# Sparse-attention heads: values stationary in half of TensorE's columns, probabilities scaled first and moving, the result already transposed

## The chip, the cores and the metric

The kernel runs on one core of one Trainium2 chip, as a single launch. The metric is device time in microseconds (us). Three runs of the kernel before took 1006.0, 1002.8 and 1006.0 us; the median is 1006.0.

## What is computed

Two transformer blocks, one after the other, on 256 tokens of width 1024 in float32. The first has a state-space mixer, a latent attention and a gated FFN; nothing in it is changed. The second has two attention mixers side by side (a sparse one, called NSA, with 12 heads, and a dilated one with 12 heads), gates, output projections and a squared-relu FFN.

The change lies in the NSA mixer. Its 12 query heads are in 3 groups of 4; a group shares one key and value head of width 64 for each of three branches:

- compressed: 15 block summaries of keys and values;
- selected: with 256 tokens there are only 4 blocks of 64 and all of them are selected, so this is plain causal attention;
- window: the window of 512 covers all 256 tokens, so this too is plain causal attention, with keys and values of its own.

For each head `y = gate0 * o_cmp + gate1 * o_slc + gate2 * o_win`, where each `o` is `softmax(q k^T * scale) v`. The 12 heads' `y` (768 columns) then goes through `w_o_a`.

## The kernel before

All weights are streamed from HBM in blocks of up to 128x2048 float32, in two halves. Each half lands in `wraw` (3 buffers); ScalarE (ACT) rounds it to `whi`, VectorE (DVE) makes `wlo = wraw - whi` (5 buffers each). A product is then three float32r matmuls (hi*hi, hi*lo, lo*hi), accumulated in PSUM in a tile named `pa` (token-major, 128x384 or 128x512 moving) or `pb` (channel-major, 128x256 moving). These make up most of the program, and their activations are `hTh` and `hTl`.

Attention is done in plain float32. In the NSA part (lines 1511 to 1573, tile names in brackets) the program goes over 3 groups `g` and, in each, over 4 heads `r`:

- scores of both branches w = 0 (selected) and 1 (window), for token tiles tt = 0 and 1, in one PSUM tile (`psN`), mask and row maximum on DVE, exponential on ACT into `pr2` (the page writes `pr`), with the row sums in `dens`;
- the probabilities are transposed on TensorE (`trp2`, page `trp`): 6 transposes of 128x128 a head, copied out to `pT2` (page `pT`) by ACT or DVE;
- 6 matmuls a head (L1554 to 1559) with the transposed probabilities (128 keys x 128 tokens) stationary and the values `vtok` (page `vsw`, 64 columns) moving, into `po`: two PSUM tiles a group, token-major, each branch and head apart.

At the end of a group (L1560 to 1573) the sums are inverted and multiplied by the gates; for each token tile DVE multiplies `po` by that factor into `yt` (512 columns), adds the two branches (256 columns) and adds the compressed branch `yc` into `yA` (256 columns). `yc` comes from `pcv`: the compressed probabilities `pcm`, transposed (`trpc`, `pcT`), times the block-diagonal values `vbd`, two matmuls of 256 columns a group, copied out by ACT. `yA` is transposed by 4 more transposes a group (`trya`) and split into `yATh`, `yATl` for the output projection.

The order of the instructions is made by a planner, `_Plan` (L518 to 794). The program is first run dry; each instruction is noted with its engine, operands and an estimated length (`_cost`, L561 to 577). Then a list schedule is made: each engine takes, of the instructions whose operands and buffers are there, the one of the lowest rank. Ranks come from the table `RANK` (L40 to 48) by the stage's name: "nsa" by group, "cmp" for the block compression, "dil" for the dilated heads. A `copy` may go to ACT or DVE, whichever is free in the plan. All instructions are issued from one helper, hence one line number for all in the profile: L629.

PSUM has 8 banks in two tags: "acc" with 3 (`pa`, `pb`, `po`) and "g" with 5 (transposes and scores).

Of the kernel before, what the change touches and what calls it, by code (L numbers as in the profile page):

```python
# [9 lines left out]
F32 = mybir.dt.float32  # L10
# [7 lines left out]
P = 128  # L18
# [13 lines left out]
NARENA = 54  # L32
WRAW = 3
# [18 lines left out]
# ---------------------------------------------------------------- host layout  # L52
# [23 lines left out]
def _weights():  # L76
    """Blocks of the weight stream: (key, width, source array, builder)."""
# [89 lines left out]
def _consts():  # L167
    """Small constants: (key, width, builder of [128, width])."""
# [81 lines left out]
# ---------------------------------------------------------------- device side  # L250
# [9 lines left out]
class _Noted(Exception):  # L260
    """Leaves the context of the dry run before anything of it is compiled."""
# [20 lines left out]
def _body(plan, x_in, wts, cst, out):  # L282
# [6 lines left out]
    # ---- storage  # L289
    def a2(name, dtype=F32):  # L290
        return plan.tile("arena", [P, 512], dtype, name, "a", NARENA)

# [20 lines left out]
    # ---- weight stream  # L313
# [22 lines left out]
    # ---- constants and input  # L336
# [24 lines left out]
    # the tensor engine's clock rises with work: turned over until the input is there  # L361
# [15 lines left out]
    # ---- pieces  # L377
# [40 lines left out]
    def gain_T(xs, gain, name):  # L418
        """Transposes token-major k-tiles and multiplies them by their gains."""
# [8 lines left out]
    def norm_T(x, r, gain, name):  # L428
        """The normed x, transposed; r [P, 2]: the norm's factors per token."""
# [7 lines left out]
    def late_T(x, gain, name):  # L437
        """The gained x, transposed, and the mean squares per token [P, 2], by which the products with x are normed."""
# [13 lines left out]
    def spread(r):  # L452
        """Factors per token [P, 2] as a row [P, 256] on every partition."""
# [11 lines left out]
    def mmA(ps, act, tt, k0, nk, w, n, woffs, start, stop):  # L465
        """ps[128 tok, n] += act^T W for k-tiles k0.., weights block w at woffs(k)."""
# [9 lines left out]
    def mmB(ps, act, w, nk, woffs, k0=0):  # L476
        """ps[128 ch, 256 tok] = W^T act over nk k-tiles."""
# [8 lines left out]
    def chunkA(keys, act, n, kper):  # L486
        """Full-K token-major chunk over several blocks; returns the two psum tiles."""
# [16 lines left out]
    def mask_max(s, mask, mx):  # L504
        """s += mask, with the rows' maxima."""
# [13 lines left out]
class _Plan:  # L519
    """The order of the instructions. A first, dry run of the program notes every instruction with its engine, its  # L520
    length and what it reads and writes. From that a list schedule is made: each engine takes, of the instructions
    whose operands and buffers are there, the one of the lowest rank. The real run gives each instruction its place
    in that schedule as its priority."""
# [6 lines left out]
    # -- the dry run  # L530
# [16 lines left out]
    def either(self, *two):  # L547
        """An instruction that one of two engines runs."""
# [12 lines left out]
    def _cost(eng, op, outs, ins):  # L561
# [5 lines left out]
        if eng == "PE":  # L567
            n = outs[0].free_size()
            if op == "transpose":
                return max(n / 1.2, 107.0) + 2.5  # L570
            return (2 * max(n / 1.2, 107.0) if ins[0].dtype == F32 else max(n / 2.4, 107.0)) + 2.5
# [41 lines left out]
    # -- the real run  # L613
# [64 lines left out]
    def _run(self, graph, seq):  # L678
        """One pass; returns its length and every instruction's start. seq: the places of the weight blocks."""
# [117 lines left out]
class _Eng:  # L797
    """An engine whose instructions the plan notes. queue: the engine that starts it, where that is another."""
# [17 lines left out]
def _rope(V, dst, src, tc_, ts_, H, half, ta, tb):  # L816
    """dst[:, h, :] = rotated src[:, h, :]; tables [p, 2*half] with the gains folded in."""
# [8 lines left out]
def block1(env):  # L826
# [5 lines left out]
    # constants worked out on the chip  # L832
# [391 lines left out]
    # ---- FFN with the depthwise convolution  # L1224
# [33 lines left out]
def block2(env, x2):  # L1258
# [5 lines left out]
    # rope tables with the gains  # L1264
# [44 lines left out]
    def headnorm(ss, n):  # L1309
        """The factors of the heads' norms [P, 2 * n], the row's own included."""  # L1310
# [8 lines left out]
    # ---- compressed keys and values: transposed, second copy shifted by one token  # L1319
# [18 lines left out]
    # ---- selected and window keys  # L1338
# [71 lines left out]
    # ---- block compression  # L1410
# [100 lines left out]
    # ---- NSA by groups of four heads  # L1511
    yAT = S.hl("yAT", 3)
    for g in range(3):
        S.rank("nsa", g)
        yA = a2("yA").rearrange("p (t d) -> p t d", t=NTT)
# [5 lines left out]
        pcv = ps_s("pcv")  # L1521
        for tt in range(NTT):
            PE.matmul(pcv[:, tt * 256:(tt + 1) * 256], pcT[:, tt * P:(tt + 1) * P],
                      vbd[g].rearrange("p r d -> p (r d)"), start=True, stop=True)
        yc = a2("yc")
        S.copy(yc, pcv)
        den = small("dens", 16)
        denv = den.rearrange("p (t w h) -> p t w h", t=NTT, w=2)
        po = [S.ps_acc("po") for _ in range(NTT)]
        pov = [p_.rearrange("p (w h d) -> p w h d", w=2, h=4) for p_ in po]  # L1530
        for r in range(4):
            h = 4 * g + r
            prob = [a2("pr2") for _ in range(2)]
            for tt in range(NTT):
                nk = P * (tt + 1)
                s = ps_s("psN")[:, :2 * nk].rearrange("p (w b) -> p w b", w=2)
                for i in range(2):
                    PE.matmul(s, qT[h][:, tt * P:(tt + 1) * P], kT[g][i][:, :, 0:nk], start=i == 0, stop=i == 1)
                mx = small("mx2", 2)
                for w in range(2):  # L1540
                    S.mask_max(s[:, w], S.mcaus[:, 2 * P - nk:], mx[:, w:w + 1])
                nb = small("nb2", 2)
                V.tensor_scalar(nb, mx, sclA[:, h, tt:tt + 1], -1.0, op0=OP.mult, op1=OP.mult)
                for w in range(2):
                    A.activation(prob[tt][:, w * nk:w * nk + nk], s[:, w], AF.Exp, bias=nb[:, w:w + 1], scale=sclA[:, h, tt:tt + 1],
                                 accum_out=denv[:, tt, w, r:r + 1])
            pT = [a2("pT2") for _ in range(2)]
            for tt in range(NTT):
                pt = ps_tr("trp2")
                n = 256 * (tt + 1)  # L1550
                for i in range(n // P):
                    PE.transpose(pt[:, i * P:(i + 1) * P], prob[tt][:, i * P:(i + 1) * P], ident)
                S.copy(pT[tt][:, :n], pt[:, :n])
            for w in range(2):  # L1554
                vs = slice(g * 64, g * 64 + 64)
                PE.matmul(pov[0][:, w, r], pT[0][:, w * P:(w + 1) * P], vtok[w][0][:, vs], start=True, stop=True)
# [3 lines left out]
        V.reciprocal(den, den)  # L1560
        for w in range(2):
            V.tensor_tensor(denv[:, :, w], denv[:, :, w], gv[:, :, 4 * g:4 * g + 4, 1 + w], op=OP.mult)
        for tt in range(NTT):
# [5 lines left out]
        pt = ps_tr("trya").rearrange("p (a b) -> p a b", a=2)  # L1569
        for j in range(2):  # L1570
            for tt in range(NTT):
# [177 lines left out]
```

## Time and profile before

| what | value |
|---|---|
| three runs | 1006.0, 1002.8, 1006.0 us |
| span of the profiled execution | 1000.4 us |
| time around the span, by the median | 5.6 us |
| PE (TensorE) busy | 988.1 us, 99% |
| DVE busy | 782.5 us, 78% |
| ACT busy | 608.0 us, 61% |
| DMA, mean | 166 GB/s |
| NSA part, first score to last `po` matmul | 597 to 745 us |

The page gives the span of the profiled execution, from its first instruction to its last; the time of a run also has what lies around it, 2.4 to 5.6 us by the three runs. A float32 matmul appears as two records of the same shape, since TensorE makes two passes over it; a transpose and a float32r matmul appear as one. A record's duration is the time from its start until its results are written; the next one starts long before that, so what a matmul costs is the distance from its start to the next start, which the timeline shows: for n merged records, (merged time - one record) / (n - 1).

### The profile page before, as it was taken

Reading aid. Unit: us, or ns where it says so; the run is one execution under the profiler, and the core shown is the slowest. Engines: PE = TensorE matmul, PEld = TensorE weight load, DVE = VectorE, ACT = ScalarE, POOL = GpSimd, SP = SyncE. Lnnn points to the kernel's source line nnn. Section 1 sums busy time; section 2 is a strip of 40 time slices with the busy share of each in tenths; the row PEclk is TensorE's granted clock in tenths of the full one; section 3 lists DMA queues with packets and bytes.
Section 4 is the critical chain, followed back from the end, with each engine's and each line's share of the span. In section 5 each row is a group of like instructions: output and inputs, shape, how many; then the busy total and the mean of one; then the engine's idle time right before and its main releaser. Section 6 shows DMA issues by size and latency. Waiting matters only on the chain.

```text
span 1000.4 us, 18303 instructions
## 1 busy us (share of the span) xinstructions
PE 988.1 (99%) x6873; PEld 926.9 (93%) x6873; DVE 782.5 (78%) x1774; ACT 608.0 (61%) x1193; POOL 0.2 (0%) x4
## 2 busy tenths in 40 slices
PE   8999999999999999999999999999999999999998
PEld 7899988999999899999888998999989989998886
DVE  6897989989876779999855999989974866665442
ACT  5755879768644566666644767765674456554331
POOL 0000000000000000000000000000000000000000
PEclk9999999999999999999999999999999999999999
DMA  7655643235435455555555654365412645555561
GB/s 246 230 178 169 202 155 139 86 120 202 145 130 186 173 183 185 180 189 181 200 189 155 182 158 145 109 211 176 135 44 80 200 170 199 181 188 182 186 223 64
DMA packets 50536, 166.44 MB, mean 166 GB/s; under 512 B 5616, under 2 KB 6928, under 8 KB 50320
## 3 DMA queue, kind: packets, MB, share of 16 engines
q1 hardware_dynamic: 50448, 165.28, 49.1%
q8 instruction: 54, 0.88, 0.3%
q14 instruction: 34, 0.28, 0.1%
HBM read 164.18 MB, written 1.08 MB: 165 GB/s over the span
## 4 chain that ended last, share of the span: by engine, by line
PE 91%; DMA 3%; DVE 3%; ACT 1%; issue 1%; SPq 0%; DVEq 0%; ACTq 0%
PE pb L629 46%; PE pa L629 30%; DMA wraw<-in_wts_dram 3%; PE trp L629 2%; DVE wlo L629 1%; PE pob L629 1%; PE po L629 1%; PE py L629 1%; PE psS L629 1%; PE pov L629 1%; PE psD L629 1%; ACT whi L629 1%; PE psN L629 1%; PE trn L629 1%; PE trq L629 1%
## 5 line engine op out<-in xcount | busy, mean ns | idle before, releaser
L629 ACT ACTIVATE whi<-wraw 128x1024 fp32r<-128x1024 f32 (+3 forms) x318 | 321.3, 1011 | 290.4 <-PE pb L629 140.1
L629 DVE TENSOR_TENSOR wlo<-wraw,whi 128x1024 fp32r<-128x1024 f32 (+3 forms) x318 | 368.7, 1161 | 161.2 <-ACT whi L629 153.1
L629 PE MATMUL pb<-hTl,whi 128*128 128x256 f32 x1056 | 300.3, 285 | 0.0
L629 PE MATMUL pb<-hTh,whi 128*128 128x256 f32 x1056 | 300.1, 285 | 0.0
L629 PE MATMUL pb<-hTh,wlo 128*128 128x256 f32 x1056 | 300.0, 284 | 0.0
L629 PEld LDWEIGHTS pb<-hTl,whi 128*128 128x128 f32 x1056 | 202.4, 192 | 0.8 <-issue 0.6
L629 PEld LDWEIGHTS pb<-hTh,whi 128*128 128x128 f32 x1056 | 202.2, 192 | 0.8 <-issue 0.6
L629 PEld LDWEIGHTS pb<-hTh,wlo 128*128 128x128 f32 x1056 | 202.5, 192 | 0.4 <-issue 0.3
L629 PE MATMUL pa<-whi,uTh 128*128 128x512 f32 x216 | 84.2, 390 | 0.0
L629 PE MATMUL pa<-wlo,uTh 128*128 128x512 f32 x216 | 84.1, 390 | 0.0
L629 PE MATMUL pa<-whi,uTl 128*128 128x512 f32 x216 | 84.0, 389 | 0.0
L629 PE MATMUL pa<-wlo,hTh 128*128 128x384 f32 (+2 forms) x224 | 79.8, 356 | 0.0
L629 PE MATMUL pa<-whi,hTh 128*128 128x384 f32 (+2 forms) x224 | 79.5, 355 | 0.0
L629 PE MATMUL pa<-whi,hTl 128*128 128x384 f32 (+2 forms) x224 | 78.8, 354 | 0.0
L629 PEld LDWEIGHTS pa<-whi,uTl 128*128 128x128 f32 x216 | 40.6, 188 | 8.4
L629 PEld LDWEIGHTS pa<-wlo,uTh 128*128 128x128 f32 x216 | 40.5, 188 | 8.4
L629 PEld LDWEIGHTS pa<-whi,uTh 128*128 128x128 f32 x216 | 40.5, 188 | 8.3
L629 PEld LDWEIGHTS pa<-whi,hTl 128*128 128x128 f32 x224 | 42.2, 189 | 1.9
L629 PEld LDWEIGHTS pa<-whi,hTh 128*128 128x128 f32 x224 | 42.1, 188 | 1.9 <-ACT vbt L629 0.2
L629 PEld LDWEIGHTS pa<-wlo,hTh 128*128 128x128 f32 x224 | 42.1, 188 | 1.8
L629 DVE SCALAR_TENSOR_TENSOR fcv<-fpr,call,fcv 128x254 f32<-128x254 f32 (+1 forms) x88 | 38.5, 478 | 0.3 <-ACT fcv L629 0.3
L629 PE MATMUL pb<-ysTl,whi 128*128 128x256 f32 x128 | 37.1, 290 | 0.0
(397 smaller groups left out, 1752.3 us busy)
## 6 DMA issues: line engine op xcount, KB each, us to landing
wraw<-in_wts_dram SPq DMA_DIRECT2D x250, 512.0 KB, 4.2
wraw<-in_wts_dram SPq DMA_DIRECT2D x52, 384.0 KB, 3.2
dec<-aD SPq DMA_DIRECT2D x16, 256.0 KB, 5.4
wraw<-in_wts_dram SPq DMA_DIRECT2D x8, 256.0 KB, 2.7
wraw<-in_wts_dram SPq DMA_DIRECT2D x4, 448.0 KB, 4.3
wraw<-in_wts_dram SPq DMA_DIRECT2D x4, 420.0 KB, 3.8
call<-in_cst_dram SPq DMA_DIRECT2D x1, 1076.5 KB, 8.4
out_dram<-yo SPq DMA_DIRECT2D x3, 256.0 KB, 4.1
```

The costliest lines, as they stand in the source:

```text
L629: getattr(engines[eng], op)(*[swap(a) for a in args], **{k: swap(a) for k, a in kw.items()})
```

## The change

Four things are changed. The rest of the diff takes out comments and docstrings, which moves lines (the helper is L636 after).

1. The NSA heads are taken in pairs `j`. The sums of a head are inverted and multiplied by its gates as soon as its exponentials are done, and the probabilities are multiplied by that factor, in place, before they are transposed (`S.copy` with a scale, ACT or DVE). The same 6 transposes a head follow, now 3 to a PSUM tile and branch; the copies go to `pT2`, now a tile of 2 x 384 columns with 3 buffers of its own.
2. The values `vtok[w][kb][:, vs]` (64 columns) are the stationary operand. The transposed probabilities move: for key block kb = 0 all 256 tokens, for kb = 1 the later 128. Head 0 of the pair writes partitions 0 to 63 of `y`, head 1 partitions 64 to 127, so each matmul takes one half of the array's columns. Both branches and the compressed one (`vbd` stationary, `pcT` moving, 128 columns wide) accumulate in the same PSUM tile, which holds the transposed result and is split at once. `yt`, `yA`, `yc`, `pcv` and `trya` are gone.
3. The rank of "cmp" goes from 41.24 to 40.9.
4. `_cost` takes a float32 matmul whose stationary operand has 64 columns or 64 partitions as half as long as before.

```diff
+NPT = 3
...
-    "in2": [39.8, 45.14, 45.06, 55.07, 49.45], "cmp": [41.24], "nsa": [41.09, 41.19, 49.84], "qb": [46.71, 41.14],
+    "in2": [39.8, 45.14, 45.06, 55.07, 49.45], "cmp": [40.9], "nsa": [41.09, 41.19, 49.84], "qb": [46.71, 41.14],
...
+    def pt_tile(name):
+
+        return plan.tile("arena", [P, 2, 384], F32, name, "pT", NPT)
...
+            if ins[0].dtype == F32 and (ins[0].free_size() == 64 or ins[0].ap[0][1] == 64):
+                return n / 1.2 + 2.5
...
-        pcv = ps_s("pcv")
-        for tt in range(NTT):
-            PE.matmul(pcv[:, tt * 256:(tt + 1) * 256], pcT[:, tt * P:(tt + 1) * P],
-                      vbd[g].rearrange("p r d -> p (r d)"), start=True, stop=True)
-        yc = a2("yc")
-        S.copy(yc, pcv)
...
-        po = [S.ps_acc("po") for _ in range(NTT)]
...
+        y = S.ps_acc("po").rearrange("p (a b) -> p a b", a=2)
+        for j in range(2):
+            probs = []
+            for r in (2 * j, 2 * j + 1):
...
+                V.reciprocal(den, den)
+                V.tensor_tensor(denv, denv, gv[:, :, h, 1:3], op=OP.mult)
+                for tt in range(NTT):
+                    nk = P * (tt + 1)
+                    for w in range(2):
+                        S.copy(prob[tt][:, w * nk:w * nk + nk], prob[tt][:, w * nk:w * nk + nk], denv[:, tt, w:w + 1])
+                probs.append(prob)
+
+            PE.matmul(y[:, j], vbd[g][:, 2 * j:2 * j + 2].rearrange("p r d -> p (r d)"), pcT[:, :T], start=True, stop=False)
+            vs = slice(g * 64, g * 64 + 64)
+            for w in range(2):
+                pT = S.pt_tile("pT2")
                 for i in range(2):
...
+                    pt = ps_tr("trp2")
+                    for n, (tt, o) in enumerate(((0, w * P), (1, 2 * w * P), (1, (2 * w + 1) * P))):
+                        PE.transpose(pt[:, n * P:(n + 1) * P], probs[i][tt][:, o:o + P], ident)
+                    S.copy(pT[:, i], pt[:, :384])
...
                 for kb in range(2):
-                    o = w * 256 + kb * P
-                    PE.matmul(pov[1][:, w, r], pT[1][:, o:o + P], vtok[w][kb][:, vs], start=kb == 0, stop=kb == 1)
...
-        for tt in range(NTT):
-            t = a2("yt")
-            tv = t.rearrange("p (w h d) -> p w h d", w=2, h=4)
-            V.tensor_tensor(tv, pov[tt], denv[:, tt][:, :, :, None].to_broadcast([P, 2, 4, 64]), op=OP.mult)
-            V.tensor_tensor(t[:, :256], t[:, :256], t[:, 256:], op=OP.add)
-            V.tensor_tensor(yA[:, tt], t[:, :256], yc[:, tt * 256:(tt + 1) * 256], op=OP.add)
...
+                    for i in range(2):
+                        PE.matmul(y[64 * i:64 * i + 64, j, kb * P:], vtok[w][kb][:, vs],
+                                  pT[:, i, 2 * kb * P:(2 + kb) * P], start=False, stop=w == 1 and kb == 1)
+        S.split(yAT[g], y)
```

Up to some 600 us the built programs are the same on every engine. On PE, late in the NSA part of the kernel before, `po` matmuls (128 stationary columns, 64 moving) stand in small lots between transposes of the next heads:

```order
L629 MATMUL pb<-hTl,whi 128x256
L629 MATMUL po<-vsw,pT_9433 128x64 x2
L629 MATMUL trp_9451<-call,pr_9256 128x128 x3
L629 MATMUL po<-vsw,pT_9443 128x64 x4
L629 MATMUL trp_9464<-call,pr_9456 128x128 x2
L629 MATMUL trp_9451<-call,pr_9256 128x128
L629 MATMUL po<-vsw,pT_9448 128x64
```

On PE in the changed kernel, where the first group's results are formed, `vbd` (full width) opens each pair's half of `po`, and 8 matmuls on half the columns follow it, the two heads of the pair in turn:

```order
L636 MATMUL trpc<-call,pcm 128x128
L636 MATMUL po<-pcT,vbd 128x256
L636 MATMUL po<-pT_7975,vsw 64x256 x2
L636 MATMUL po<-pT_7975,vsw 64x128 x2
L636 MATMUL po<-pT_7988,vsw 64x256 x2
L636 MATMUL po<-pT_7988,vsw 64x128 x2
L636 MATMUL po<-pcT,vbd 128x256
L636 MATMUL po<-pT_8129,vsw 64x256 x2
L636 MATMUL po<-pT_8129,vsw 64x128 x2
L636 MATMUL po<-pT_8617,vsw 64x256 x2
L636 MATMUL po<-pT_8617,vsw 64x128 x2
L636 MATMUL trpc<-call,pcm 128x128
```

A `po` row says how many partitions are written (64 or 128) and how many columns move. The 48 half-width matmuls stand in 13 such unbroken stretches: three of 8, one each of 7, 4 and 3, three of 2 and four single ones. The `psD` matmuls (dilated scores, 64 rows) stand in 9 unbroken stretches before and in 7 after. All of group 0 now comes behind the block compression, since its accumulation begins with the compressed branch.

On DVE, at the first heads of the changed kernel, the inversion, the gates and the scaling stand between the score masks, the weights' low parts and the block compression (`hs`):

```order
L636 RECIPROCAL dens<-dens 128x4
L636 TENSOR_SCALAR nb_7933<-mx_7906,sclA 128x2
L636 TENSOR_TENSOR dens<-dens,gv 128x4
L636 ISA psN,mx_7912<-psN,mcaus 128x128
L636 ISA mx_7912 128x1
L636 TENSOR_SCALAR pr_7856<-pr_7856,dens 128x128
L636 TENSOR_SCALAR pr_7895<-pr_7895,dens 128x256
L636 TENSOR_TENSOR wlo<-wraw,whi 128x768
L636 TENSOR_SCALAR hs<-hs 128x180
```

Of the 48 scalings, 30 fall to DVE (17 of 128 columns, 13 of 256) and 18 to ACT (7 and 11).

## Rows read from the trace of the kernel before

**Rows 1.** The page, part 1: busy us (share of the span), instructions.

```profile
PE 988.1 (99%) x6873; PEld 926.9 (93%) x6873; DVE 782.5 (78%) x1774; ACT 608.0 (61%) x1193; POOL 0.2 (0%) x4
```

**Rows 2.** The page, part 4: the chain that ended last, by engine.

```profile
PE 91%; DMA 3%; DVE 3%; ACT 1%; issue 1%; SPq 0%; DVEq 0%; ACTq 0%
```

**Rows 3.** Busy time by stretch: stretch, us, PE, PEld, DVE, ACT, POOL, PEclk, DMA share, GB/s.

```profile
575.00:725.00 150.00, 146.97 (x1023) 141.25 (x1022) 141.37 (x453) 98.28 (x208) 0.00 (x0) 1.00 0.49 156
725.00:775.00 50.00, 50.00 (x398) 46.83 (x397) 30.09 (x103) 29.67 (x82) 0.00 (x0) 1.00 0.20 61
700.00:725.00 25.00, 25.00 (x193) 23.44 (x192) 24.19 (x95) 16.15 (x38) 0.00 (x0) 1.00 0.42 140
```

**Rows 4.** Waits of PE from 595 to 765: waited for, total us, times, longest.

```profile
PE trp L629 <- DVE qT L629: 0.9, 1, 0.9
PE po L629 <- ACT pT L629: 0.8, 2, 0.6
PE trq L629 <- DVE qT L629: 0.6, 1, 0.6
```

**Rows 5.** PE from 595 to 765, by shape: count, busy us, mean ns, idle before.

```profile
L629 PE MATMUL po<-vsw,pT 128*128 128x64 f32 x144 | 18.6, 270 | 0.8 <-ACT pT L629 0.8
L629 PE MATMUL pcv<-vbd,pcT 128*128 128x256 f32 x12 | 3.0, 388 | 0.0
```

**Rows 6.** Timeline of PE: start us, merged us, instruction, count.

```profile
629.83 3.68 PE L629 MATMUL po<-vsw,pT 128*128 128x64 f32 x32
...
713.59 1.89 PE L629 MATMUL pcv<-vbd,pcT 128*128 128x256 f32 x8
...
716.69 0.62 PE L629 MATMUL trya<-call,yA 128*128 128x128 f32 x4
```

**Rows 7.** Timeline of PE around matmuls of 64 rows (`psD`).

```profile
722.31 0.28 PE L629 MATMUL pb<-hTh,whi 128*128 128x256 f32 x1
722.52 0.93 PE L629 MATMUL psD<-qT,qT 64*128 64x128 f32 x6
...
723.61 0.28 PE L629 MATMUL pb<-hTh,wlo 128*128 128x256 f32 x1
```

**Rows 8.** Timeline of PE around matmuls of 45 and of 32 columns.

```profile
645.50 0.28 PE L629 MATMUL ph<-wlo,kps 128*45 128x256 f32 x1
645.62 0.28 PE L629 MATMUL ph<-whi,kps 128*90 128x256 f32 x1
645.74 0.28 PE L629 MATMUL ph<-wlo,kps 128*45 128x256 f32 x1
...
89.30 0.38 PE L629 MATMUL tra<-call,acum 128*32 128x128 f32 x2
89.43 0.48 PE L629 MATMUL pa<-whi,hTh 128*128 128x512 f32 x1
89.75 0.40 PE L629 MATMUL pa<-wlo,hTh 128*128 128x512 f32 x1
```

**Rows 9.** DVE from 590 to 765, by shape.

```profile
L629 DVE TENSOR_TENSOR yt<-po,dens 128x512 f32<-128x512 f32 x6 | 4.1, 686 | 0.4 <-PE po L629 0.2
L629 DVE TENSOR_TENSOR yt<-yt 128x256 f32<-128x256 f32 x6 | 2.5, 418 | 0.0
L629 DVE TENSOR_TENSOR yA<-yt,yc 128x256 f32<-128x256 f32 x6 | 2.3, 417 | 0.0
L629 DVE TENSOR_TENSOR dens<-dens,gv 128x8 f32<-128x8 f32 x6 | 0.8, 164 | 0.1
L629 DVE RECIPROCAL dens<-dens 128x16 f32<-128x16 f32 x3 | 0.8, 252 | 0.9 <-ACT pr L629 0.9
L629 DVE RECIPROCAL rdb<-rdb 128x8 f32<-128x8 f32 x1 | 0.2, 203 | 0.0
```

**Rows 10.** ACT, the same stretch.

```profile
L629 ACT ACTIVATE yc<-pcv 128x512 f32<-128x512 f32 x3 | 1.7, 595 | 0.8 <-PE pcv L629 0.8
```

**Rows 11.** Tiles `qn` and `junk`, nearest to the scalings: shortest, median, longest ns.

```profile
L629 DVE TENSOR_SCALAR qn<-qkv,ny x4: 283/316/349, 47.5 to 48.2; 128x256 f32<-128x256 f32 x2, 128x128 f32<-128x128 f32 x2
L629 ACT ACTIVATE junk<-qkv x6: 212/304/456, 27.5 to 35.0; 128x256 f32<-128x256 f32 x2, 128x128 f32<-128x128 f32 x2, 128x32 f32<-128x32 f32 x2
```

More of the change, by code (lines that the diff above doesn't have):

```diff
@@ L260 @@
 class _Noted(Exception):
+    pass
 def _net(tc, x_in, wts, cst, out):
@@ L1514, in block2 @@
         S.rank("nsa", g)
-        yA = a2("yA").rearrange("p (t d) -> p t d", t=NTT)
         ptc = ps_tr("trpc")
@@ L1520, in block2 @@
         S.copy(pcT[:, :256], ptc[:, :256])
-        pcv = ps_s("pcv")
-        for tt in range(NTT):
-            PE.matmul(pcv[:, tt * 256:(tt + 1) * 256], pcT[:, tt * P:(tt + 1) * P],
-                      vbd[g].rearrange("p r d -> p (r d)"), start=True, stop=True)
-        yc = a2("yc")
-        S.copy(yc, pcv)
-        den = small("dens", 16)
-        denv = den.rearrange("p (t w h) -> p t w h", t=NTT, w=2)
-        po = [S.ps_acc("po") for _ in range(NTT)]
-        pov = [p_.rearrange("p (w h d) -> p w h d", w=2, h=4) for p_ in po]
@@ L1531, in block2 @@
-        for r in range(4):
-            h = 4 * g + r
-            prob = [a2("pr2") for _ in range(2)]
-            for tt in range(NTT):
-                nk = P * (tt + 1)
-                s = ps_s("psN")[:, :2 * nk].rearrange("p (w b) -> p w b", w=2)
-                for i in range(2):
[L1538 to L1556, printed above, removed]
-                for kb in range(2):
-                    o = w * 256 + kb * P
-                    PE.matmul(pov[1][:, w, r], pT[1][:, o:o + P], vtok[w][kb][:, vs], start=kb == 0, stop=kb == 1)
@@ L1560, in block2 @@
[L1560 to L1563, printed above, removed]
-            t = a2("yt")
-            tv = t.rearrange("p (w h d) -> p w h d", w=2, h=4)
-            V.tensor_tensor(tv, pov[tt], denv[:, tt][:, :, :, None].to_broadcast([P, 2, 4, 64]), op=OP.mult)
-            V.tensor_tensor(t[:, :256], t[:, :256], t[:, 256:], op=OP.add)
-            V.tensor_tensor(yA[:, tt], t[:, :256], yc[:, tt * 256:(tt + 1) * 256], op=OP.add)
@@ L1569, in block2 @@
-        pt = ps_tr("trya").rearrange("p (a b) -> p a b", a=2)
-        for j in range(2):
-            for tt in range(NTT):
-                PE.transpose(pt[:, j, tt * P:(tt + 1) * P], yA[:, tt, j * P:(j + 1) * P], ident)
-        S.split(yAT[g], pt)
+        y = S.ps_acc("po").rearrange("p (a b) -> p a b", a=2)
+        for j in range(2):
+            probs = []
+            for r in (2 * j, 2 * j + 1):
+                h = 4 * g + r
+                prob = [a2("pr2") for _ in range(2)]
+                den = small("dens", 4)
+                denv = den.rearrange("p (t w) -> p t w", t=NTT)
+                for tt in range(NTT):
+                    nk = P * (tt + 1)
+                    s = ps_s("psN")[:, :2 * nk].rearrange("p (w b) -> p w b", w=2)
+                    for i in range(2):
+                        PE.matmul(s, qT[h][:, tt * P:(tt + 1) * P], kT[g][i][:, :, 0:nk], start=i == 0, stop=i == 1)
+                    mx = small("mx2", 2)
+                    for w in range(2):
+                        S.mask_max(s[:, w], S.mcaus[:, 2 * P - nk:], mx[:, w:w + 1])
+                    nb = small("nb2", 2)
+                    V.tensor_scalar(nb, mx, sclA[:, h, tt:tt + 1], -1.0, op0=OP.mult, op1=OP.mult)
+                    for w in range(2):
+                        A.activation(prob[tt][:, w * nk:w * nk + nk], s[:, w], AF.Exp, bias=nb[:, w:w + 1], scale=sclA[:, h, tt:tt + 1],
+                                     accum_out=denv[:, tt, w:w + 1])
+                V.reciprocal(den, den)
+                V.tensor_tensor(denv, denv, gv[:, :, h, 1:3], op=OP.mult)
+                for tt in range(NTT):
+                    nk = P * (tt + 1)
+                    for w in range(2):
+                        S.copy(prob[tt][:, w * nk:w * nk + nk], prob[tt][:, w * nk:w * nk + nk], denv[:, tt, w:w + 1])
+                probs.append(prob)
+            PE.matmul(y[:, j], vbd[g][:, 2 * j:2 * j + 2].rearrange("p r d -> p (r d)"), pcT[:, :T], start=True, stop=False)
+            vs = slice(g * 64, g * 64 + 64)
+            for w in range(2):
+                pT = S.pt_tile("pT2")
+                for i in range(2):
+                    pt = ps_tr("trp2")
+                    for n, (tt, o) in enumerate(((0, w * P), (1, 2 * w * P), (1, (2 * w + 1) * P))):
+                        PE.transpose(pt[:, n * P:(n + 1) * P], probs[i][tt][:, o:o + P], ident)
+                    S.copy(pT[:, i], pt[:, :384])
+                for kb in range(2):
+                    for i in range(2):
+                        PE.matmul(y[64 * i:64 * i + 64, j, kb * P:], vtok[w][kb][:, vs],
+                                  pT[:, i, 2 * kb * P:(2 + kb) * P], start=False, stop=w == 1 and kb == 1)
```

## The prediction

> **What bounds the kernel.** First the page's busy times: TensorE (PE) is busy in 99% of the span, DVE in 78%, ACT in 61% [rows 1]. Then the chain that ended last: 91% of it is PE, 3% DMA, 3% DVE [rows 2]. So the time is the sum of what PE issues, and the reader should ask of each edit how many PE slots it takes. Third, the stretch in which the NSA heads lie, since the chain is an average: from 575 to 725 us PE is busy 147 of 150 us, but DVE 141.4 of 150, and in its fullest slice 24.19 of 25 (96.8%); from 725 to 775 DVE has fallen to 30 of 50 [rows 3]. Fourth, what PE truly waits for there: 0.9, 0.8 and 0.6 us are the longest of five such entries [rows 4]. The granted clock is 1.00, the higher level (2.4 GHz), in all of it [rows 3]. PE is the bound, DVE a close second up to 725 us.
>
> **PE work taken away.** The 72 matmuls on the values are 144 passes [rows 5]. Thirty-two of them in a row took 3.68 us, so one takes (3.68 - 0.27) / 31 = 0.110 us [rows 5, 6], although only 64 columns move: 15.8 us. The six `pcv` matmuls are 12 passes [rows 5] of (1.89 - 0.39) / 7 = 0.214 us [rows 5, 6]: 2.6 us. Twelve transposes `trya` at (0.62 - 0.28) / 3 = 0.113 us, a record taken as the 0.28 us of its neighbours [rows 6, 7]: 1.4 us. Together 19.8 us.
>
> **PE work added.** The six `vbd` matmuls move 256 columns at full width: 12 passes of 0.214 us, 2.6 us. The new value matmuls are 24 of 256 and 24 of 128 moving columns, two passes each. At 0.214 and 0.11 us a pass (a 128-column pass has no row without a start-up in it; half of 0.214 is 0.108, and 64 columns already take 0.110) they come to 10.3 + 5.3 = 15.6 us if no two run together. That is one end: 19.8 - 2.6 - 15.6 = 1.6 us less. The other end is that the two halves of the array work side by side throughout: 7.8 us, so 9.4 us less.
>
> No row shows two halves of the columns at work together; the nearest, six `psD` matmul passes in one half of the rows, go one after the other, but they use the same half [rows 7]. I take the overlap, since the code puts two heads in turn on different columns, into different partitions of PSUM, and a start in all of these rows waits for the streaming before it and not for its result (records of 0.27 us start 0.11 us apart [rows 6]). But I don't take all of it. Matmuls stay in order, and the two passes of one matmul use the same half. So I went through the 13 stretches of the new order pass by pass, each starting when the one before has started and its own half is free: 1.62 us for each of the three stretches of eight (2.6 us one after the other), 1.41, 0.97 and 0.65 for those of 7, 4 and 3, 2.9 for the seven short ones: 10.8 us. Less by 19.8 - 2.6 - 10.8 = 6.4 us.
>
> The Trainium skill (TensorE: Matmul & The Clock Gate, section "Measured speedup vs the span model") gives 2.38 times for three column tiles of 512 columns. No run here shows it. An estimate by that page, the same 79% of the ideal for two tiles, would be 15.6 / 1.59 = 9.8 us in place of 10.8.
>
> **Change of the array's shape.** Going from full width to 64 rows and back has a price in this trace: from a `pb` at 722.31 over six `psD` passes to the second `pb` behind them at 723.61 are 1.30 us, where 2 x 0.12 + 6 x 0.11 = 0.90 would do: 0.40 us for both ways [rows 7]. `psD` stands in two stretches fewer: 0.8 us less. Going from full width to 45 columns and back costs nothing: `ph` rows alternate every 0.12 us. Nor does 32 columns: two `tra` and the `pa` behind take 0.45 us to the next start, which is 2 x 0.11 and one 512-column slot of 0.23 [rows 8]. The new stretches narrow the columns, not the rows, so by the nearest row I take nothing; the other end is 13 x 0.40 = 5.2 us.
>
> The Trainium skill (TensorEngine Tiling (Array Packing), section "Key Properties") says against this change that a change of tiling mode drains TensorE. By that rule the forecast would be 5.2 us later; the trace agrees for rows and not for columns.
>
> **DVE and ACT.** Gone from DVE: `yt` 4.1 and 2.5, `yA` 2.3, the sums' gates and inversions 0.8 and 0.8: 10.5 us [rows 9]. New: 12 inversions of 4 columns at 0.20 (the row with 8), 12 gate products at 0.16 [rows 9], and 30 scalings. These have no row; the same kind of instruction takes 0.28 us at 128 columns and 0.35 at 256 [rows 11], so 17 x 0.28 + 13 x 0.35 = 9.3 us. Net +3.2 us. ACT loses `yc`, 1.7 us [rows 10], and gets 18 scalings at 0.30 and 0.46 [rows 11], 7.2 us: +5.5. The copies of transposed probabilities keep their number of columns (768 a head). All this lies under PE; the cover is thin on DVE (8.6 us free up to 725 us) and wide on ACT (98 of 150 us busy) [rows 3]. If it is gone, the DVE part costs PE its 3.2 us and what DVE can't follow of the shorter PE work (rival 3).
>
> **Waits and the earlier compression.** The first `po` of a stretch waits for a copy of `pT`, as now (0.8 us in two waits [rows 4]). Behind a waiting `po` stand, in PE's order, the other seven of its stretch and the next heads' transposes; for those wait the copies and, over the 3 `pT` buffers, the next pair. The chain before it is longer by inversion, gate and scaling. Bounds: 0.8 us less (no such wait) to 12 tiles x 0.9, the longest single wait of rows 4, 10.8 us more. Since nearly all stretches have `pa`, `pb` or transposes of other heads ahead of them, I take two more waits of 0.5 us, 1.0 us. The rank of "cmp" and the planner's halved cost only reorder work that is there anyway, and the weight blocks with it; the DMA is busy half the time [rows 3]: nothing, and the wait just named as its upper bound.
>
> **Sum.** -6.4 - 0.8 + 1.0 = -6.2 us: a span of 994.2 for the profiled 1000.4. That span was 5.6 us below the median, and I keep that distance: 1006.0 - 6.2 = 999.8 us, 0.6% faster.
>
> **Rivals.**
> 1. The array drains at each narrow stretch. For it: rows 7; against it: rows 8, though there no second half is in use. -6.2 + 5.2 = -1.0: 1005.0 us.
> 2. The halves don't run together, so the change doesn't do what it says. For it: no row shows it. -1.6 - 0.8 + 1.0 = -1.4: 1004.6 us.
> 3. DVE becomes the bound up to 725 us. For it: 141.4 of 150 us [rows 3], and 3.2 us come on top. At the share of its fullest slice, 144.6 / 0.968 = 149.4 us, so the stretch gives back 0.6 us, and the two `psD` stretches 0.8 behind it: 1004.6 us. Against it: DVE has 20 us free from 725 to 775, and work can move there.
> 4. Slower: PE stands at the head of the `po` stretches for the copies of `pT`, of which only three tiles exist, behind the longer chain. 12 x 0.9 = 10.8 us in place of 1.0: -7.2 + 10.8 = +3.6: 1009.6 us. It decides from 0.6 us a tile on (7.2 / 12). For it: the copies are shared out on a DVE that is 94% busy; against it: half of the tiles are filled long before their group starts.
>
> **Chances.** Forecast 0.45 (its own range 996 to 1003), rivals 0.20, 0.12, 0.10 and 0.13. A measurement of this kernel tells 0.5%, 5 us, from no change (three runs spread over 3.2 us). Two thirds of the forecast's share lie below 1001.0, and three tenths of the first three rivals' (any of them with one wait fewer or more overlap): 0.30 + 0.13 = 0.43 faster. Slower by 5 us is most of rival 4 and a little of 1 and 2: 0.13. The rest, 0.44, is the same. The range from 995.0 (overlap nearly full, 9.4 + 0.8 and 0.8 of waits) to 1008.5 leaves out the worse half of rival 4 and a little at the lower end.
>
> **What would show it.** Right: `po` records of the two heads that start while the other half streams, so that eight matmuls of a stretch take about 1.6 us; no extra time before a stretch or behind it; `yt`, `yA` and `trya` gone; PE busy less by some 6 us between 600 and 760. Wrong: 2.6 us a stretch (rival 2), 0.2 us before and behind each (rival 1), PE waiting for `wlo` or scores in 600 to 725 with DVE at 97% (rival 3), or waits of `po` for `pT` of more than 7 us in all (rival 4).

## The result: 0.9% slower

The changed kernel took 1013.1 us (median of 4 runs, 1011.9 to 1014.6), the kernel before on the same chip 1004.9 (4 runs). The ratio is 1.0089, with a 95% interval of 1.0070 to 1.0108. The forecast was 999.8 us, 0.6% faster; the chance given to slower by over 0.5% was 0.13.

The profiled run of the changed kernel is the slowest of its four (1014.6 us), that of the kernel before the fastest of its own (1002.8), so their spans, 1012.7 and 1000.4 us, lie 12.3 us apart where the medians lie 8.2 apart. The page of the changed kernel, part 1 (busy us, share of the span, instructions) and part 4 (the chain by engine):

```profile
PE 993.4 (98%) x6813; PEld 923.7 (91%) x6813; DVE 781.9 (77%) x1797; ACT 613.4 (61%) x1212; POOL 0.2 (0%) x4
```

```profile
PE 93%; DMA 3%; DVE 2%; ACT 1%; issue 1%; SPq 0%; DVEq 0%; ACTq 0%
```

PE has 60 instructions fewer and is 5.3 us longer busy [rows 1]. Why is seen in its busy time by stretch (as [rows 3]: stretch, us, PE, PEld, DVE, ACT, POOL, PEclk, DMA share, GB/s):

```profile
575.00:725.00 150.00, 142.07 (x926) 130.97 (x924) 137.80 (x465) 100.89 (x220) 0.00 (x0) 0.96 0.49 152
725.00:775.00 50.00, 48.20 (x329) 41.67 (x329) 29.45 (x108) 30.16 (x83) 0.00 (x0) 0.89 0.21 61
610.00:620.00 10.00, 7.71 (x24) 6.15 (x25) 9.43 (x33) 6.31 (x12) 0.00 (x0) 0.50 0.70 207
722.00:736.00 14.00, 11.29 (x45) 9.66 (x46) 7.98 (x43) 6.04 (x23) 0.00 (x0) 0.52 0.11 38
```

In the last two stretches the granted clock is 0.50, the lower level (1.2 GHz), for 10.2 us from 610.0 and for 13.7 us from 722.7; in the kernel before it was 1.00 in all of 575 to 775 [rows 3]. Ahead of the first PE had stood idle for 0.6 and 0.9 us, waiting for `wlo`. What it did before the second is in its timeline (start, us, instruction, in brackets the idle time ahead and what ended it):

```profile
722.36 0.44 PE L636 MATMUL trq<-call,qrot 128*128 128x128 f32 x2 [1.47 <-ACT pr L636]
723.27 1.65 PE L636 MATMUL psD<-qT,qT 64*128 64x128 f32 x6 [0.47 <-ACT qT L636]
726.80 1.22 PE L636 MATMUL psD<-qT,qT 64*128 64x256 f32 x2 [1.88 <-ACT pr L636]
```

It had stood idle for 1.47 us; two more waits lie inside the slow stretch. The six `psD` passes that took 0.93 us before [rows 7] take 1.65. In the first slow stretch the 384-column `pa` passes start 0.32 us apart; at full clock they start 0.17 apart:

```profile
616.30 0.53 PE L636 MATMUL pa<-whi,hTl 128*128 128x384 f32 x1
616.62 0.53 PE L636 MATMUL pa<-whi,hTh 128*128 128x384 f32 x1
...
671.75 0.34 PE L636 MATMUL pa<-wlo,hTh 128*128 128x384 f32 x1
671.92 0.34 PE L636 MATMUL pa<-whi,hTl 128*128 128x384 f32 x1
```

PE's waits from 590 to 780 (waited for, total us, times, longest), where the kernel before had none above 0.9 [rows 4]:

```profile
PE pa L636 <- ACT whi L636: 1.9, 1, 1.9
PE psD L636 <- ACT pr L636: 1.9, 1, 1.9
PE ph L636 <- DVE wlo L636: 1.5, 2, 0.9
PE trq L636 <- ACT pr L636: 1.5, 1, 1.5
PE pa L636 <- DVE rb L636: 1.2, 1, 1.2
```

These are the five largest; no `po` is among them or behind them. The new value products themselves are as wanted. First one stretch of eight between two `vbd` products (start, merged us), then all of them by shape (count of passes, busy us, mean ns):

```profile
672.73 0.60 PE L636 MATMUL po<-pcT,vbd 128*128 128x256 f32 x2
673.25 1.52 PE L636 MATMUL po<-pT,vsw 128*64 128x256 f32 x16
674.70 0.70 PE L636 MATMUL po<-pcT,vbd 128*128 128x256 f32 x2
```

```profile
L636 PE MATMUL po<-pT,vsw 128*64 128x256 f32 x48 | 9.8, 395 | 0.0
L636 PE MATMUL po<-pT,vsw 128*64 128x128 f32 x48 | 6.7, 280 | 0.0
```

### Where the 12.3 us are

Three numbers for each profiled run: what the low clock cost PE (half of its busy time in the stretches at 0.50, as those take twice as long), its busy time without that (the work), and its idle time (span less busy).

| kernel | span | PE busy | low clock | work | idle |
|---|---|---|---|---|---|
| before | 1000.4 | 988.1 | 1.7 | 986.4 | 12.3 |
| changed | 1012.7 | 993.4 | 11.3 | 982.1 | 19.3 |
| difference | +12.3 | +5.3 | +9.6 | -4.3 | +7.0 |

The 11.3 is half of 3.4 (at the start, which the kernel before has too), 7.95 and 11.3 us. It is what the low clock added to PE's busy time, not yet what it added to the span; that is measured below, by filling the idle places.

### The profile page after: what moved, and what is told of

Read it like the earlier page. It is cut to its first block, busy times and chain, and to the rows that moved or that the text cites. A ratio compares the mean times of both kernels' runs of the same rounds, so it can differ in the third digit from the quotient of the medians.

```text
span 1012.7 us, 18214 instructions
## 1 busy us (share of the span) xinstructions
PE 993.4 (98%) x6813; PEld 923.7 (91%) x6813; DVE 781.9 (77%) x1797; ACT 613.4 (61%) x1212; POOL 0.2 (0%) x4
## 4 chain that ended last, share of the span: by engine, by line
PE 93%; DMA 3%; DVE 2%; ACT 1%; issue 1%; SPq 0%; DVEq 0%; ACTq 0%
PE pb L636 46%; PE pa L636 32%; DMA wraw<-in_wts_dram 2%; PE trp L636 2%; PE po L636 1%; PE pob L636 1%; PE py L636 1%; PE psD L636 1%; PE psS L636 1%; DVE wlo L636 1%; PE pov L636 1%; PE psN L636 1%; PE trn L636 1%; ACT whi L636 1%; PE trq L636 1%; PE pq L636 1%
## 5 line engine op out<-in xcount | busy, mean ns | idle before, releaser
L636 ACT ACTIVATE whi<-wraw 128x1024 fp32r<-128x1024 f32 (+3 forms) x318 | 321.0, 1011 | 286.5 <-PE pb L636 144.9
L636 DVE TENSOR_TENSOR wlo<-wraw,whi 128x1024 fp32r<-128x1024 f32 (+3 forms) x318 | 368.6, 1162 | 160.7 <-ACT whi L636 154.0
L636 PE MATMUL pb<-hTh,whi 128*128 128x256 f32 x1056 | 301.5, 286 | 0.0
L636 PE MATMUL pb<-hTl,whi 128*128 128x256 f32 x1056 | 301.2, 286 | 0.0
L636 PE MATMUL pb<-hTh,wlo 128*128 128x256 f32 x1056 | 301.2, 285 | 0.0
L636 PEld LDWEIGHTS pb<-hTh,whi 128*128 128x128 f32 x1056 | 203.3, 193 | 2.5 <-issue 1.6
L636 PEld LDWEIGHTS pb<-hTl,whi 128*128 128x128 f32 x1056 | 203.6, 193 | 1.1 <-issue 1.0
L636 PEld LDWEIGHTS pb<-hTh,wlo 128*128 128x128 f32 x1056 | 203.7, 193 | 0.1
L636 PE MATMUL pa<-whi,uTh 128*128 128x512 f32 x216 | 84.2, 390 | 0.0
L636 PE MATMUL pa<-wlo,uTh 128*128 128x512 f32 x216 | 84.1, 390 | 0.0
L636 PE MATMUL pa<-whi,uTl 128*128 128x512 f32 x216 | 84.0, 389 | 0.0
L636 PE MATMUL pa<-whi,hTh 128*128 128x384 f32 (+2 forms) x224 | 80.5, 360 | 3.1 <-ACT whi L636 1.9
L636 PE MATMUL pa<-wlo,hTh 128*128 128x384 f32 (+2 forms) x224 | 80.5, 359 | 0.4 <-DVE wlo L636 0.4
L636 PE MATMUL pa<-whi,hTl 128*128 128x384 f32 (+2 forms) x224 | 79.5, 357 | 0.0
L636 PEld LDWEIGHTS pa<-whi,uTl 128*128 128x128 f32 x216 | 40.5, 188 | 8.5
L636 PEld LDWEIGHTS pa<-wlo,uTh 128*128 128x128 f32 x216 | 40.6, 188 | 8.4
L636 PEld LDWEIGHTS pa<-whi,uTh 128*128 128x128 f32 x216 | 40.6, 188 | 8.2
L636 PEld LDWEIGHTS pa<-whi,hTh 128*128 128x128 f32 x224 | 42.7, 191 | 5.6 <-ACT whi L636 2.3
L636 PEld LDWEIGHTS pa<-wlo,hTh 128*128 128x128 f32 x224 | 42.8, 191 | 2.7 <-DVE wlo L636 0.9
L636 PEld LDWEIGHTS pa<-whi,hTl 128*128 128x128 f32 x224 | 42.7, 191 | 2.0
L636 DVE SCALAR_TENSOR_TENSOR fcv<-fpr,call,fcv 128x254 f32<-128x254 f32 (+1 forms) x88 | 38.5, 478 | 0.3 <-ACT fcv L636 0.3
L636 PE MATMUL pb<-ysTl,whi 128*128 128x256 f32 x128 | 37.1, 290 | 0.0
```

The lines of the kernel that those rows point to most:

```text
L636: getattr(engines[eng], op)(*[swap(a) for a in args], **{k: swap(a) for k, a in kw.items()})
```

## Experiments

Theory A: the new order (the rank of "cmp" and the cost line; the planner makes another sequence) lets PE stand idle, and its clock falls. Theory B: the scaling does it, by its work on DVE and ACT and its longer chain. Others asked what the fall of the clock costs by itself, whether the two halves work together, and whether the edit gains in another order.

### Each cause alone, in the kernel before

```
-    ... "cmp": [41.24], ...
+    ... "cmp": [40.9], ...
```

> The kernel before with one number changed: the rank of 'cmp' is 40.9 in place of 41.24, as in the changed kernel; no instruction is added or taken away. Theory A (the order: the compression's weight blocks and sums come earlier, TensorE stands still near them for several us, and its clock falls for a stretch): at least one stretch between 580 and 640 us with 3 us or more of idle TensorE, a granted clock of 0.5 for some 10 us behind it, and 1008 to 1015 us. Theory B (the scaling of the probabilities, by its work on DVE and ACT and its longer chain, makes the waits): no such stretch, clock 0.998, 1003 to 1007 us.

Measured: 1016.8 us, ratio 1.0127 [1.0094, 1.0160], above both ranges. One number, with no instruction added or taken away (three copies go to ACT in place of DVE), costs as much as the whole change. The clock is at 0.50 for 3.4 us at 634, 13.7 at 679 and 3.4 at 744; the stretch around the longest:

```profile
675.00:700.00 25.00, 23.27 (x123) 22.73 (x122) 17.28 (x59) 10.40 (x27) 0.00 (x0) 0.73 0.15 46
```

A holds in the main: the clock falls and the time is far from B's 1003 to 1007. But where A named its stretch the clock is low for 3.4 us only, and the longest slow stretch lies 40 us behind it.

```
             pT = [a2("pT2") for _ in range(2)]     # ahead of this, per head:
+            V.reciprocal(rsv, denv[:, :, :, r])
+            V.tensor_tensor(rsv, rsv, gv[:, :, h, 1:3], op=OP.mult)
+            ... S.copy(prob[tt][...w...], prob[tt][...w...], rsv[:, tt, w:w + 1])   # tt, w
```

> The kernel before, with ranks and costs untouched, and the scaling added: per head a reciprocal and a product of 4 columns, and 4 copies of the probabilities with a scale, ahead of the transposes (the rows are divided again behind the values, so the output is divided twice). TensorE's instructions are those of before. Theory A (order): the scaling lies beside TensorE's work, no new stretch at half clock, 1004 to 1007 us. Theory B (scaling): TensorE waits 3 us or more in a row somewhere between 600 and 730 us, the granted clock falls to 0.5 there, 1010 to 1020 us.

Measured: 1019.2 us (1013.5 to 1024.7), ratio 1.0154 [1.0099, 1.0210], with 13.7 us at 0.50 between 663 and 701. B holds in the main too (the longest single wait is 2.8 us, not 3). But the added instructions were noted by the planner, so the order changed with them: this run can't tell the copies' work from the order that the planner makes of it.

### The changed kernel with another rank, with and without the scaling

```
-    ... "cmp": [40.9], ...
+    ... "cmp": [39], ...
```

> The changed kernel with the rank of 'cmp' at 39 in place of 40.9. Theory A (order): the idle stretch at 606 to 616 us moves or shrinks, with its stretch at half clock, and the time leaves 1013 by 3 us or more (estimate 1006 to 1010). Theory B (scaling): the waits belong to the chain of softmax, scaling, transposes; both stretches at half clock stay within 10 us of where they are, 1011 to 1015 us.

> The run of the changed kernel with rank 39 once more, with the 48 copies that scale the probabilities left out (so the probabilities reach the values unscaled). TensorE's instructions are the same. Theory A (order): within 3 us of the run with rank 39. Theory B (scaling): no stretch at half clock between 600 and 740 us, and 997 to 1001 us, which is 1005 less the 6 to 7 us that the values' edit saves.

Measured: 1023.3 us with the scaling, ratio 1.0196 [1.0167, 1.0226]; 1005.3 without, 1.0019 [0.9999, 1.0039]. The rank moves the time by 8 to 10 us, as A had it, but the wrong way, so its estimate of 1006 to 1010 missed, and so did B's 1011 to 1015. Leaving 48 copies out gives 18 us back and all the slow stretches but one of 3.4 us, which spoke for B; yet it stays 4 us above B's 997 to 1001, and again the order is another one.

### The scaling left out, the order kept

```
             eng, op, args, kw = self.calls[i][...]
+            if <a copy from pr2 to itself>: continue    # while the planned order is issued
```

> The changed kernel in exactly its own order on every engine, with only the 48 copies that scale the probabilities left out of the instruction streams (the probabilities reach the values unscaled). Theory A (it is the order, whatever the scaling): waits between 605 and 617 us and around 725 us and both stretches at half clock stay, 1011 to 1015 us. Theory B (it is the scaling's work on DVE and ACT and its place in the chain, for which this order has no room): both stretches at half clock go, the waits fall by 5 us or more, 999 to 1004 us.

Measured: 1013.4 us, ratio 1.0104 [1.0086, 1.0122]; the changed kernel gave 1.0089 and, in the repeat below, 1.0113. The waits are those of the changed kernel, and the slow stretches lie where they did (6.8 us from 612 and 13.7 from 721):

```profile
PE pa L639 <- ACT whi L639: 2.3, 1, 2.3
PE psD L639 <- ACT pr L639: 1.9, 1, 1.9
PE trq L639 <- ACT pr L639: 1.5, 1, 1.5
PE ph L639 <- DVE wlo L639: 1.5, 2, 0.9
```

```profile
721.00:735.00 14.00, 11.53 (x45) 9.81 (x46) 7.21 (x37) 5.90 (x22) 0.00 (x0) 0.51 0.11 37
```

This decides it. The copies cost nothing measurable where this order stays, although records of 16.6 us go with them (DVE is busy 4.7 us less, ACT 5.9); what they cost in the runs before came through the order that the planner made around them. Theory B falls.

### The cost line

```
-            if ins[0].dtype == F32 and (ins[0].free_size() == 64 or ins[0].ap[0][1] == 64):
+            if ins[0].dtype == F32 and ins[0].free_size() == 64:
```

> The changed kernel with the planner's shorter cost kept for products of 64 output rows or columns' worth of weights only where the second operand has 64 columns; the dilated heads' score products (64 rows) have their cost of before again. No instruction is added or taken away. Theory A (order, in which this cost line makes the second idle stretch): the waits at 722 to 728 us and the 13.65 us at half clock behind them are gone, the first stretch stays, 1004 to 1009 us. Theory B (scaling makes the waits): they stay or move by a few us, 1011 to 1016 us.

Measured: 1005.9 us (10 runs), ratio 1.0019 [1.0004, 1.0033], as A had it. The first slow stretch stays (6.8 us at 0.50 from 614), the second is gone:

```profile
725.00:750.00 25.00, 25.00 (x178) 19.69 (x178) 18.02 (x69) 18.30 (x54) 0.00 (x0) 1.00 0.16 48
```

So one of the two conditions in the cost line made the second stretch, the one for the 64-row score products of the dilated heads, which the change otherwise leaves alone: 7 us against the changed kernel's median, 9 against that of its repeat below.

### Needless work in the idle places

```
+            if i in FILL:        # issued behind planned instruction i, the order else untouched
+                for _ in range(n): engines["PE"].matmul(out, left, tiny, start=False, stop=False)
```

`tiny` is made once, by two instructions on ACT near the start.

> The changed kernel with its order untouched and 47 needless products added on TensorE at the six places between 605 and 617 us where it stood idle: each adds 1e-20 times 'kps' onto the open accumulation 'ph' (256 columns, 0.117 us each at full clock, 5.5 us of work in all), sized a little under the wait that they lie in. Theory A with the clock (idle TensorE makes the clock fall, and the fall costs more than the wait): the granted clock stays at 1.00 from 600 to 640 us, the time falls by 3 to 4 us although work is added (half of the 7.8 us that TensorE was busy at half clock), to 1009 to 1010; the second stretch at 722 us stays as it is. Rival (the waits alone cost, or the clock falls for another reason): the stretch at half clock stays, time the same or up to 1 us longer.

> The changed kernel once more, beside the filled one on the same chip: 1012 to 1014 us, stretches at half clock behind 610 and 722 us.

> The changed kernel with its order untouched and 9 needless products added on TensorE at the three places between 722 and 728 us where it stood idle before its second stretch at half clock (each adds 1e-20 times 'vbd' onto the open accumulation 'po': 256 columns in two passes, 0.43 us, 3.9 us in all, against waits of 5.1 us). Around 725 to 750 us DVE and ACT are busy only 55% of the time, so here TensorE alone sets the pace. Theory A with the clock: the granted clock stays at 1.00 from 720 to 745 us and the time falls by 4 to 5 us (half of the 8.3 to 11.3 us that TensorE was busy at half clock there), to 1010 to 1011; the first stretch, behind 610 us, stays. Rival (the fall of the clock costs nothing by itself, as filling the first stretch suggests): within 2 us of the changed kernel, 1013 to 1016.

Measured: 1015.3 us for the changed kernel again, ratio 1.0113 [1.0094, 1.0132]; 1014.5 with the first place filled, 1.0108 [1.0089, 1.0128]; 1009.9 with the second, 1.0064 [1.0047, 1.0082]. In both the granted clock stays at 1.00 where the filling is and still falls at the other place. First place filled, 610 to 620; then the second place, in the repeat and filled:

```profile
610.00:620.00 10.00, 8.14 (x50) 6.55 (x49) 8.37 (x32) 6.00 (x12) 0.00 (x0) 1.00 0.64 192
```

```profile
725.00:750.00 25.00, 22.65 (x127) 17.11 (x126) 14.48 (x62) 14.15 (x45) 0.00 (x0) 0.80 0.12 38
```

```profile
725.00:750.00 25.00, 25.00 (x167) 19.32 (x165) 16.97 (x74) 16.43 (x49) 0.00 (x0) 1.00 0.11 38
```

So at either place, once its idle time is filled, the clock doesn't fall. Idle time alone is not always enough, though: in the run with the scaling alone TensorE stood idle for the same 1.47 us, and the clock stayed at 1.00 (timeline and stretch). What else it takes isn't shown here.

```profile
733.10 0.55 PE L629 MATMUL trp<-call,pr 128*128 128x128 f32 x3 [1.47 <-ACT pr L629]
```

```profile
725.00:750.00 25.00, 23.53 (x176) 20.85 (x175) 20.79 (x84) 14.91 (x41) 0.00 (x0) 1.00 0.16 53
```

What the fall costs can be read from five profiled executions that have one and the same order. The first place lies between the first `ph` product behind 600 us and the first `trh` transpose, the second between that and the first `yATl` product; the starts of these three, and the distances, in us:

| run | `ph`, `trh`, `yATl` | first place | of it at 0.50 | second place | of it at 0.50 |
|---|---|---|---|---|---|
| changed | 602.06, 628.64, 774.10 | 26.6 | 10.2 | 145.5 | 13.7 |
| repeat | 604.50, 631.27, 775.21 | 26.8 | 6.8 | 143.9 | 10.2 |
| first place filled | 600.86, 627.51, 771.47 | 26.7 | 0 | 144.0 | 10.2 |
| second place filled | 603.71, 629.95, 770.50 | 26.2 | 6.8 | 140.6 | 0 |
| order kept, no scaling | 600.87, 627.64, 772.87 | 26.8 | 6.8 | 145.2 | 13.7 |

At the second place the fall costs 3.4 us where it lasts 10.2, and 4.7 to 4.9 where it lasts 13.7: over four fifths of half of PE's busy time there (4.2 and 5.7). With 3.9 us of work added the kernel is 3 to 5 us faster by the medians (1009.9, against 1013.1 and 1015.3 for the changed kernel and, on the same chip, 1013.4 with the order kept).

At the first place neither the fall nor the filling shows: the five lie within 0.6 us, whatever the clock. There the rival was right about the time (the medians are 0.8 us apart, inside their intervals), but not about the clock, which it expected to fall again. The profiled executions of the pair are 3.8 us apart, but the filled one was 3.6 us ahead before it came there. The chain that ended last shows what may hide the fall (start, us, what; the longest pieces): from 602 to 615.8 us it runs over a block of weights, from its transfer to its parts `whi` and `wlo`, and comes back to PE only then.

```profile
602.24 5.22 DMA wraw<-in_wts_dram
607.57 1.07 ACT whi L636
610.16 1.14 DVE wlo L636
615.82 3.25 PE pa L636 x9
```

So a faster PE would only come sooner to weights that aren't split yet; that this is the reason is argued, not tested.

With this the table's 12.3 us read otherwise. Of the 9.6 only the second place is a price, some 4.8 us; PE's work gives 4.3 back; so waiting makes up the rest, 12.3 - 4.8 + 4.3 = 11.8 us (an estimate), part of it hidden in the table behind a PE that was slow where it would have stood idle. The waits cost more than the clock.

### The two halves

```
-                        PE.matmul(y[64 * i:64 * i + 64, j, kb * P:], ...
+                        PE.matmul(y[64 * (i * w * kb):64 * (i * w * kb) + 64, j, kb * P:], ...
```

> The changed kernel with head 1 of a pair written to the same half of the output partitions as head 0 (all but its last product, so 3 of 4 pairs of products can't lie side by side; head 1's part is added onto head 0's rows, which leaves the output wrong there). Same plan, same instructions and places. If the two halves do run side by side: each of the 6 stretches of 8 products takes 0.43 + 0.22 + 0.43 = 1.08 us more, 6.5 us in all (estimate, from a 256-column product of two passes at 0.216 us), so 1018 to 1021 us. If they don't: within 1.5 us of the changed kernel, 1012 to 1015 us.

Measured: 1020.1 us, ratio 1.0161 [1.0141, 1.0181], so 5 to 7 us above the changed kernel. The value products by shape:

```profile
L636 PE MATMUL po<-pT,vsw 128*64 128x256 f32 x48 | 13.5, 391 | 0.0
L636 PE MATMUL po<-pT,vsw 128*64 128x128 f32 x48 | 8.3, 281 | 0.0
```

21.8 us in place of 16.5. The halves do run side by side.

### Another order for the same work

The ranks were searched anew on the planner's own schedule, for few and short idle times of TensorE; the second run also issues the `vbd` product behind the value products of a pair.

```
-    ... "cmp": [40.9], "nsa": [41.09, 41.19, 49.84], "qb": [46.71, 41.14],
+    ... "cmp": [39.15], "nsa": [51.815, 41.196, 49.747], "qb": [48.369, 54.161],
...
-            if ins[0].dtype == F32 and (ins[0].free_size() == 64 or ins[0].ap[0][1] == 64):
+            if ins[0].dtype == F32 and ins[0].free_size() == 64:
```

> The changed kernel with the scaling, the values' products and the buffers as they are; only numbers are changed: 24 ranks of the second layer's steps, and the cost line as in the run on the cost. In this order TensorE is given other work where it stood still. Theory A (order): no stretch at half clock between 550 and 780 us, idle time of TensorE back to about 12 us as before, so 1003 (the kernel before on this chip) less the 4.3 us of work that TensorE has less, 997 to 1001 us. Theory B (the 48 copies for the scaling cost by themselves, by their work on DVE and ACT): 1005 to 1013 us, whatever the order.

> The same with the compression's product issued behind the 8 products of the values of a pair of heads instead of ahead of them (it closes the accumulation that it opened), with ranks of its own. Theory A: no stretch at half clock between 550 and 780 us, 996 to 1001 us. Theory B: 1005 to 1013 us.

Measured: 999.6 us (7 runs, 996.4 to 1002.7), ratio 0.9949 [0.9933, 0.9965], for the first; 1008.8, 1.0045 [1.0030, 1.0060], for the second. The first beats both kernels, with all the scaling in it. Its page, part 1, two stretches, and its value products:

```profile
PE 983.7 (99%) x6813; PEld 917.3 (92%) x6813; DVE 782.6 (78%) x1795; ACT 614.2 (62%) x1214; POOL 0.2 (0%) x4
```

```profile
575.00:725.00 150.00, 146.05 (x999) 133.83 (x998) 136.76 (x451) 107.38 (x239) 0.00 (x0) 1.00 0.48 146
725.00:775.00 50.00, 50.00 (x391) 46.96 (x390) 37.41 (x131) 29.04 (x73) 0.00 (x0) 1.00 0.42 125
```

```profile
L636 PE MATMUL po<-pT,vsw 128*64 128x256 f32 x48 | 9.6, 392 | 0.0
L636 PE MATMUL po<-pT,vsw 128*64 128x128 f32 x48 | 6.6, 276 | 0.0
```

Work is 980.2 us (983.7 less 3.4), idle 13.9 of a span of 997.6. (The 3.4 is half of two slow stretches of 3.4 us in the first 60 us. All 27 ranks of the second layer's steps differ, not the 24 that were expected.) The second has no slow stretch there either (clock 1.00), as A had it, but its time misses A's range and lies in B's. That is not B's reason, as its value products tell:

```profile
L636 PE MATMUL po<-pT,vsw 128*64 128x256 f32 x48 | 13.8, 399 | 0.0
L636 PE MATMUL po<-pT,vsw 128*64 128x128 f32 x48 | 9.4, 283 | 0.0
```

23.2 us in place of 16.2, and PE's work is 988.4, 8.2 more. Without the `vbd` product to wait for, the planner issues the products of a pair as their operands come, with `pb` and transposes between the heads: 19 stretches in the trace where the first run has 9, so fewer pairs side by side and more changes of shape.

## Why the prediction was wrong

**The step that failed** is the last of its costs: the rank and the halved cost "only reorder work that is there anyway [...]: nothing, and the wait just named as its upper bound", and with it the 1.0 us for waits. The rank alone cost 1.3% in the kernel before; the cost line 7 to 9 us in the changed one. The prediction looked for the price of a wait at the instruction that the edit touches (`po` for `pT`, of which there is none), and the idle time came at `ph`, `pa`, `trq` and `psD`, products and transposes that it had counted, if at all, as cover. By the estimate above the waits cost some 11.8 us more than before, where it took 1.0. It also read "The granted clock is 1.00" as a given, and set no price on its loss; that loss turned 3.8 us of idle time at 721 to 727 into some 8.6, and the run without that place gained 7 to 9.

**PE's work** went the right way, by 4.3 us where -6.4 and -0.8 were forecast. The overlap is better than the pass-by-pass walk had it: from the first start to the end of the last slot eight products take 1.35 us (1.52 less the last record's 0.27, and 0.10 for its slot), not 1.62 (2.6 one after the other). The walk let the second head begin only when both passes of the first had started; in the trace the first passes of the two heads start together, two records of 0.43 us in 0.44:

```profile
673.25 0.44 PE L636 MATMUL po<-pT,vsw 128*64 128x256 f32 x2
```

The Trainium skill (TensorE: Matmul & The Clock Gate, section "Measured speedup vs the span model") led to an estimate of 1.59 times for two tiles; here 2.6 / 1.35 is 1.9 times, with the start-up of the stretch inside.

**The change of shape** was taken as nothing, by the nearest row of 45 columns, and that was the wrong row. From one `vbd` to the next are 1.97 us (672.73 to 674.70) for 0.43 of `vbd` and, at 0.209 and 0.103 us between starts in the stretch, 1.25 of value products: 0.3 us for both ways, and the `vbd` behind is 0.1 longer (0.70, not 0.60). A single product, in one half alone, pays too:

```profile
686.72 0.33 PE L636 MATMUL pa<-whi,hTh 128*128 128x384 f32 x1
686.98 0.65 PE L636 MATMUL po<-pT,vsw 128*64 128x256 f32 x2
687.56 0.55 PE L636 MATMUL trp<-call,pr 128*128 128x128 f32 x3
```

From the `pa` to the transposes are 0.84 us for slots of 0.17 and 2 x 0.21, so 0.25 for both ways. At 0.25 to 0.39 us the 13 stretches cost 3 to 5 us, an estimate; rival 1 had 5.2, and its sign, extra time before and behind each stretch, is there. That is the 2.9 us by which PE's work falls short of the forecast, and what the better overlap gives. The Trainium skill (TensorEngine Tiling (Array Packing), section "Key Properties") says that a change of mode drains TensorE; the trace now agrees for stretches of 64 columns, with 0.25 to 0.39 us, and still not for 45 and 32 columns [rows 8].

**DVE and ACT** were sized well: scalings 8.7 us on DVE (9.3 forecast) and 7.9 on ACT (7.2), inversions and gates 3.8 (4.3). That they are hidden was right, as the run with the order kept shows; rivals 2, 3 and 4 did not happen as described. Of rival 3 a sign is there, PE waiting for `wlo` with DVE busy 9.4 of 10 us at 610 to 620, but not its reason: these waits stay when the scalings are gone. Rival 4 came nearest in sign and size (1009.6), by a mechanism that isn't the one measured.

**What stays open:** why the clock fell behind one idle time of 1.5 us and not behind another, and why the orders that the planner found good leave TensorE waiting at just these places.

## What to carry over

Where a planner orders the work, an edit is two changes, of the work and of the order: keep one fixed when the other is timed (here by leaving instructions out of an order already made), or the cost of the order is put down to the instruction. Price the waits of TensorE first, wherever the new order puts them, and then what they do to the granted clock behind them: of the two falls here only one cost time, so look at what the chain runs over there. Then search the order anew for the new work, and keep products that share the array next to each other.

## What was not expected of the hardware

- TensorE fell to 1.2 GHz for 13.7 us behind a single idle time of 1.5 us, though not behind every one as long; 3.9 us of needless products there made the kernel 3 to 5 us faster. Ten us at that clock elsewhere cost nothing that shows.
- Two float32 products in different halves of the columns keep their full pace together (256 columns every 0.21 us in each half), but a stretch of them, even of a single one, costs 0.25 to 0.39 us to enter and to leave.
